# Hybrid decoder layer: products of ones before the first transposes, two tiles of x split straight from PSUM, memory's squares taken earlier

## The chip, the core and the metric

The kernel runs on one core of a Trainium2 chip. A core has TensorE (PE in the profile, with its weight loads as PEld), VectorE (DVE), ScalarE (ACT), GpSimd (POOL) and SyncE (SP, which here only issues DMAs). PE multiplies from the on-chip memory SBUF into the accumulators in PSUM; ACT and DVE read both; DMA moves data between SBUF and the chip's main memory. The metric is the device time of one execution in microseconds (us), the median of several.

## What is computed

One layer of a decoder on x (1024 tokens of 2048 channels, float32) with 256 memory tokens:

```python
h = rmsnorm(x, ln_g)
proj = h @ w_in                                   # split into 11 column groups
out_a = gmlp_spatial_gating(g_u, g_v, ...) * silu(g_z)
o = gated_delta_rule(q, k, v, g, beta)            # 8 heads, after a short causal convolution
out_b = rmsnorm(o, dn_norm_g) * silu(d_z)
m = rmsnorm(mem, mem_norm_g)
mk, mv = split(m @ w_mem_kv)                      # keys and values of memory, 4 heads x 128
out_c = softmax(c_q @ mk.T / sqrt(128)) @ mv * silu(c_z)
x = x + concat(out_a, out_b, out_c) @ w_out
y = rmsnorm(x, final_g)
```

## The kernel before

**Arithmetic.** Products that need float32 accuracy are made from pairs. A tensor is split into a high part, rounded to the fast type float32r by an ACT cast, and a low part, the difference taken by DVE (`split_to`, L440). A product is then three fast products, high x high, high x low and low x high (`triple`, L463). The split weights are called whi and wlo, the split normed x is ahi and alo: 16 tiles of 128 channels by 512 tokens, held as four tensors each (`ahq`, `alq`). A few small products and all transposes are done in plain float32.

**An order written by a planner.** The program does not issue instructions directly. Each call is recorded as an `Op` with an engine, a modelled cost and the ops that it must follow (L138). At the end `Plan.issue` (L228) simulates the five engines: whenever an engine is free it takes, among the ops that are ready by the model, the one with the lowest rank, and with equal ranks the one that stands first in the program. `rank(n)` sets the rank (default 5, products 9), `behind(op)` makes everything inside wait for an op. The result is a fixed order for each engine, which then runs in that order. All instructions are recorded by one helper, so the profile gives L295 for nearly every row; tiles are told apart by name.

**Two halves.** The sequence is treated in halves of 512 tokens, each of four tiles of 128 tokens. The first half's normed x is in ahi/alo from the start; the second half's is made later (`prep1`, L734), stored in main memory (`hT_d`), and loaded into ahi/alo when the first half's projections are over (`refill`, L1205). The raw first half is also kept in main memory (`h0_d`), because the later block products (a scheme that forms sums and differences of blocks and so needs seven block products instead of eight) use sums of the two halves: `left_sums` (L720) loads four raw 128x512 blocks into the ring zg, forms sums and differences on DVE and stores them to `s_d`.

**The first 70 us.** Memory's keys and values are computed first. Loads go out in this order: memory's rows (into tiles of the rings kT and qT), its norm gains, the weight rows of w_mem_kv (four buffers kvraw, made of the rings wraw and ut). A transpose turns the gains into a column (gcol, L532 to L536). Then 16 steps k follow (L580): ACT makes the scaled high part of the weights (whi, two buffers), DVE the low part (wlo), and PE runs 18 products, 12 of 256 columns into the four banks acc and 6 of 512 columns into two banks of dn. Memory's rows are transposed as they are, four channel tiles at a time (`spread_mem`, L537); their norm is a row factor rm, applied at the end. It comes from `row_scale` (L472): four squares with accumulation on ACT, all written to the one scrap tile jk, two small DVE ops, and a power on POOL. It is called for both memory tiles at k = 5, behind tile 0 of x.

Between the steps the four x tiles of the first half are prepared by `prep` (L548): row_scale, then for each quarter of the channels a DVE multiplication by scale and gains (gb, which lie in the ring zg), four PE transposes into one of two PSUM banks (`spare`, L528), and `put0` (L564), which copies the bank to a tile of the ring tn on ACT (rank 1), splits that copy into ahq and alq (rank 2), and stores it to `h0_d` (rank 6). Tiles 0, 1 and 2 are prepared at k = 5, 9 and 13, tile 3 after the last step.

**After that.** `project_first` (L836) makes the first projection, the tokens of tiles 0 and 1 first. Then each convolution of a head (`conv`, L860) runs one projection of 48 products of 512 columns, evacuates it, and takes a tile of the ring tn for a tanh on ACT. At each such convolution one job is taken from the list `todo` (`next_job`, L845): four `prep1`, which each take four tn tiles (`keep_rows`, L559), then four `left_sums`. Eight convolutions (heads 0 to 3, q and k) empty these eight jobs; four value projections and then `refill` follow. The ring tn has four tiles, handed out in the order of the program.

Of the kernel before, what the change touches and what calls it, by code (L numbers as in the profile page):

```python
# [12 lines left out]
ALU = mybir.AluOpType  # L13
# [4 lines left out]
P = 128  # L18
D = 2048
KT = D // P  # L20
# [3 lines left out]
NT = HT // P  # L24
# [36 lines left out]
class Plan:  # L61
# [27 lines left out]
    @contextmanager  # L89
    def rank(self, cls):  # L90
        old, self.cls = self.cls, cls
        yield
        self.cls = old

    @contextmanager
    def behind(self, op):
        old, self.gate = self.gate, op
        yield
        self.gate = old
# [199 lines left out]
def kernel(  # L299
# [21 lines left out]
    x, mem, w_in, out = x[0], mem[0], w_in[0], out[0]  # L321
# [7 lines left out]
    V, S, G, PE, Q = R.dve, R.act, R.pool, R.pe, R.sp  # L329
    rank, behind = R.rank, R.behind  # L330

    def C(shape, name, dt=F32):
        return sb.tile(list(shape), dt, name=name, tag=name)[:]

    def DT(shape, name, dt=F32):
        return dr.tile(list(shape), dt, name=name, tag=name)[:]
# [41 lines left out]
    def tok(ap):  # L378

        return ap.rearrange("p (t c) -> p t c", c=P)  # L380
# [3 lines left out]
    ahq = [C([P, NT, 4, P], f"ahi{q}", F32R) for q in range(NQ)]  # L384
    alq = [C([P, NT, 4, P], f"alo{q}", F32R) for q in range(NQ)]
    for t in (*ahq, *alq):
        R.users[t.tensor.name] = []
    ahi = [ahq[k // 4][:, :, k % 4] for k in range(KT)]
    alo = [alq[k // 4][:, :, k % 4] for k in range(KT)]
# [9 lines left out]
    ring = {t: Slots(t, 4, [P, HT]) for t in ("kT", "qT", "vs", "kd", "ai")}  # L399
# [13 lines left out]
    turn = {"acc": 0, "tp": 0, "dn": 0}  # L413
# [5 lines left out]
    def tpb():  # L419
        turn["tp"] += 1  # L420
        return acc[2 + turn["tp"] % 2]

    h0_d = DT([KT, P, HT], "h0d")
    hT_d = DT([KT, P, HT], "hTd")


    ident, ones, utri = (C([P, P], n) for n in ("ident", "ones", "utri"))
    G.memset(ident, 0.0)
    G.affine_select(out=ident, in_=ident, compare_op=ALU.not_equal, fill=1.0, base=0,
                    pattern=[[-1, P]], channel_multiplier=1)  # L430
    G.memset(ones, 1.0)
    mhalf = C([P, 8], "mhalf")
    G.memset(mhalf, -0.5)

    def rsqrt_to(o, a):
        with rank(1):
            G.tensor_tensor(out=o, in0=a, in1=mhalf[:, : a.shape[1]], op=ALU.pow)


    def split_to(hi, lo, src, eng):  # L440
        S.copy(hi, src)
        eng.tensor_tensor(out=lo, in0=src, in1=hi, op=ALU.subtract)
# [29 lines left out]
    def row_scale(xq):  # L472

        s = small()
        for c in range(4):
            S.activation(jk, xq[c], AF.Square, accum_out=s[:, c : c + 1])
        V.tensor_reduce(s[:, 4:5], s[:, 0:4], axis=AX.X, op=ALU.add)
        V.tensor_scalar(s[:, 4:5], s[:, 4:5], 1.0 / D, EPS, op0=ALU.mult, op1=ALU.add)
        rsqrt_to(s[:, 5:6], s[:, 4:5])
        return s[:, 5:6]  # L480


    def row_tiles(tag):
        if tag in ("inv", "gt", "ut"):
            return [b[:, i * HT : (i + 1) * HT] for b in (ring[tag](), ring[tag]()) for i in range(2)]
        return [ring[tag]() for _ in range(4)]
# [3 lines left out]
    mem_rows = [row_tiles("kT"), row_tiles("qT")]  # L490
# [6 lines left out]
    def kv_parts(k):  # L497
        n = XW if k == 0 else 2 * XW
        return [slice(i, i + n) for i in range(0, 2 * XW, n)]

    def load_kv(k):
        for sl in kv_parts(k):
            Q.dma_start(kvraw[k % 4][:, sl], w_mem_kv[k * P : (k + 1) * P, sl])

    def load_x(tt, tag, after=(None,) * 4):
        x_rows[tt] = row_tiles(tag)
        for c in range(4):
            with behind(after[c] or R.gate):
                Q.dma_start(x_rows[tt][c], x[tt * P : (tt + 1) * P, c * HT : (c + 1) * HT])
# [18 lines left out]
    def spare():  # L528
        turn["dn"] = 1 - turn["dn"]
        return flip[turn["dn"]]  # L530

    pt = spare()  # L532
    PE.transpose(pt[:, 0:16], mrow, ident[0:16, 0:16])
    gcol = C([P, 16], "gcol")
# [24 lines left out]
    def keep_rows(dst, q, tt, tp):  # L559
        t = ring["tn"]()  # L560
        S.copy(t, tp.rearrange("p t c -> p (t c)"))
        Q.dma_start(dst[4 * q : 4 * q + 4, :, tt * P : (tt + 1) * P].rearrange("k p n -> p k n"), tok(t))

    def put0(tt):  # L564
        def put(q, tp):
            t = tok(ring["tn"]())
            with rank(1):
                S.copy(t, tp)
            with rank(2):
                split_to(ahq[q][:, tt], alq[q][:, tt], t, V)  # L570
            with rank(6):
                Q.dma_start(h0_d[4 * q : 4 * q + 4, :, tt * P : (tt + 1) * P].rearrange("k p n -> p k n"), t)

        return put


    rm = []
    kvmark = []
    mhl = [spread_mem(0)]
    for k in range(KT):  # L580
        mh, ml = mhl[k // 4]
        if k >= 4:
            with rank(3):
                load_kv(k)
        hi, lo = kvhi[k % 2], kvlo[k % 2]
        with rank(2):
            for sl in kv_parts(k):
                raw = kvraw[k % 4][:, sl]
                S.activation(hi[:, sl], raw, AF.Copy, scale=gcol[:, k : k + 1])
                V.scalar_tensor_tensor(lo[:, sl], raw, gcol[:, k : k + 1], hi[:, sl], op0=ALU.mult, op1=ALU.subtract)  # L590
        kk = k % 4
        for h in range(NX):
            sl = slice(h * P, (h + 1) * P)
            triple(ka[h][:, :NMEM], (hi[:, sl], lo[:, sl]), (mh[:, kk], ml[:, kk]), k == 0, k == KT - 1)
        for mt in range(2):
            sl = slice(mt * P, (mt + 1) * P)
            triple(va[mt], (mh[:, kk, sl], ml[:, kk, sl]), (hi[:, XW:], lo[:, XW:]), k == 0, k == KT - 1)
        kvmark.append(R.ops[-1])
        if k == 3:
            with rank(2), behind(kvmark[-1]):  # L600
                for c in range(4):
                    Q.dma_start(gb[c], ln_g[0, c * HT : (c + 1) * HT].partition_broadcast(P))
        if k in (1, 4, 8):
            with behind(kvmark[-1]):
                mhl.append(spread_mem(len(mhl)))
        if k == 1:
            load_x(0, "vs", kvmark[1:2] * 4)
        if k == 4:
            load_x(1, "kd", kvmark[4:5] * 4)
        if k == 5:  # L610
            prep(0, put0(0), spare)
            for mt in range(2):
                rm.append(C([P, 1], f"rm{mt}"))
                V.tensor_copy(rm[mt], row_scale(mem_rows[mt]))
        if k == 7:

            dg, rmb = (ring["E"]()[:, 0:NMEM] for _ in range(2))
            for mt in range(2):
                V.tensor_scalar(dg[:, mt * P : (mt + 1) * P], ident, rm[mt], None, op0=ALU.mult)
            pt = spare()  # L620
            PE.matmul(pt[:, 0:NMEM], ones, dg, start=True, stop=True)
            S.copy(rmb, pt[:, 0:NMEM])
        if k == 9:
            prep(1, put0(1), spare)
            load_x(2, "kT", (kvmark[6], kvmark[7], kvmark[7], kvmark[8]))
        if k == 13:
            load_x(3, "qT", (kvmark[10], kvmark[11], kvmark[11], kvmark[12]))
            with rank(2):
                prep(2, put0(2), spare)
# [6 lines left out]
    for mt in range(2):  # L636
        t = [ring["ai"](F32R) for _ in range(2)]
# [9 lines left out]
    for h in range(NX):  # L647
        t = ring["vs"](F32R).rearrange("p (s m) -> p s m", s=2)
# [48 lines left out]
    NJ = NH // 2  # L697
# [19 lines left out]
    def blk(w, k, c0):  # L717
        return w[k * P : (k + 1) * P, c0 : c0 + HT]

    def left_sums(j):  # L720
        a, b, c, d = (ring["zg"]() for _ in range(4))
        with rank(6):
            for t, x_ in zip((c, d, a, b), (hT_d[j], hT_d[NH + j], h0_d[j], h0_d[NH + j])):
                Q.dma_start(t, x_)
            V.tensor_tensor(out=d, in0=c, in1=d, op=ALU.add)
            Q.dma_start(s_d[0][j][0], d)
            V.tensor_tensor(out=c, in0=a, in1=c, op=ALU.subtract)
            Q.dma_start(s_d[0][j][2], c)
            V.tensor_tensor(out=d, in0=d, in1=a, op=ALU.subtract)
            Q.dma_start(s_d[0][j][1], d)  # L730
            V.tensor_tensor(out=b, in0=b, in1=d, op=ALU.subtract)
            Q.dma_start(s_d[0][j][3], b)

    def prep1(i):  # L734
        load_x(NT + i, "ut")
        prep(NT + i, lambda q, tp: keep_rows(hT_d, q, i, tp), over(scan_banks))
# [77 lines left out]
    todo = []  # L814
# [379 lines left out]
    decays(0, a)  # L1194
    R.late = R.LATE
    todo += [lambda i=i: prep1(i) for i in range(NT)]
    todo += [lambda j=j: left_sums(j) for j in range(NJ)]
    gdrs = [front(0, 0, (first, None)), front(1, 0)]
    for h in range(NJ):
        early_values(h, 0)  # L1200
# [4 lines left out]
    def refill(k):  # L1205

        raw = wraw()
        with rank(2):
            Q.dma_start(raw, hT_d[k])
            split_to(ahi[k], alo[k], tok(raw), V)  # L1210

    a = tpb()

    def before(k):
# [369 lines left out]
    for n, (tag, to) in enumerate((("gt", mkT), ("inv", mv))):  # L1584
        for i in range(NX // 2):
            t = ring[tag](F32R).rearrange("p (h s m) -> p h s m", h=2, s=2)
# [103 lines left out]
    tn = ring["tn"].bufs  # L1690
# [86 lines left out]
```

## Time and profile before

| | |
|---|---|
| median of 3 runs | 1633.85 us (1631.82 to 1637.55) |
| the profiled execution, time | 1636.6 us |
| the profiled execution, span | 1634.8 us |
| PE busy | 1611.6 us |
| DVE busy | 1259.3 us |
| ACT busy | 1029.1 us |
| mean granted PE clock | 0.997 |
| mean DMA rate over the span | 262 GB/s |

The span runs from the first to the last instruction of the core; the time of the execution holds a little more. Busy time of PE is the union of its products' modelled durations. They overlap: a product of 512 columns lasts 0.39 us in the trace while the next one starts 0.23 us after it, so how fast PE goes is read from the distance between starts. In the timeline a row gives the start, the duration, the engine, the operation, the tiles (out<-in), the shape, how many were merged, and in brackets how long the engine had been idle and what ended that. A view by windows gives busy microseconds of each engine, the number of instructions, the granted clock, and the share and rate of DMA.

### The profile page before, as it was taken

To read this page: it belongs to the slowest core of one execution; us is meant where nothing else is said; L and a number is where in the kernel's file an instruction comes from. 1 tells how busy PE (TensorE), PEld (TensorE's weight loads), DVE (VectorE), ACT (ScalarE), POOL (GpSimd) and SP (SyncE) were. 2 spreads that over 40 slices of the span, in tenths; PEclk is the share of its full clock that TensorE was granted. 3 is DMA by queue.
4 is the path that set the end of the run, shared out by engine and by line. 5 is a ranking of instruction groups with operands and counts; after the bars stand their busy time and mean duration, and the time that the engine had idled before them with its cause. 6 is when DMAs were issued, how large, how long until landed. Compare 5 with 4: busy or idle time off the path is not lost.

```text
span 1634.8 us, 26073 instructions
## 1 busy us (share of the span) xinstructions
PE 1611.6 (99%) x8562; PEld 1353.0 (83%) x8562; DVE 1259.3 (77%) x2082; ACT 1029.1 (63%) x2223; POOL 292.1 (18%) x482
## 2 busy tenths in 40 slices
PE   8999999999999999999999999999999999999997
PEld 7888888887788888888788888888888888888886
DVE  5866777878865567899898897777768888689775
ACT  6867765765365556888685356765666784344345
POOL 0011310461341110223135014231000000000001
PEclk9999999999999999999999999999999999999999
DMA  9977897899967886589878977878968879688646
GB/s 315 258 219 208 264 293 229 262 306 292 353 231 232 279 286 197 189 301 342 288 242 277 304 226 245 266 263 293 323 218 267 266 227 361 203 270 299 216 145 241
DMA packets 279146, 428.93 MB, mean 262 GB/s; under 512 B 30889, under 2 KB 104162, under 8 KB 279010
## 3 DMA queue, kind: packets, MB, share of 16 engines
q1 hardware_dynamic: 256258, 366.81, 68.4%
q0 software_dynamic: 22144, 59.40, 11.8%
q8 instruction: 67, 1.10, 0.3%
q10 hardware_dynamic: 608, 1.06, 0.2%
q14 instruction: 69, 0.57, 0.1%
HBM read 339.57 MB, written 87.06 MB: 261 GB/s over the span
## 4 chain that ended last, share of the span: by engine, by line
PE 88%; DMA 7%; ACT 2%; DVE 2%; issue 1%; SPq 0%; POOLq 0%; POOL 0%; ACTq 0%; DVEq 0%
PE acc L295 67%; PE dn L295 20%; DMA y<-in_w_in_dram 1%; DMA wraw<-in_w_in_dram 1%; ACT whi L295 1%; DMA raws<-h0d 1%; DMA ut<-in_x_dram 0%; DVE wlo L295 0%; DMA kd<-in_w_in_dram 0%; ACT jk L295 0%; DMA el<-vd 0%; DMA qT<-in_w_in_dram 0%; DMA kT<-in_w_in_dram 0%; DMA wraw<-in_w_mem_kv_dram 0%; DMA kT<-in_x_dram 0%
## 5 line engine op out<-in xcount | busy, mean ns | idle before, releaser
L295 PE MATMUL acc<-ahi,whi 128*128 128x512 f32 (+1 forms) x1512 | 534.9, 392 | 2.1 <-ACT whi L295 2.1
L295 PE MATMUL acc<-ahi,wlo 128*128 128x512 f32 (+1 forms) x1144 | 447.9, 391 | 1.0 <-DVE wlo L295 1.0
L295 PEld LDWEIGHTS acc<-ahi,whi 128*128 128x128 f32 x1512 | 283.2, 189 | 57.4 <-ACT whi L295 3.0
L295 PE MATMUL acc<-alo,whi 128*128 128x512 f32 (+1 forms) x776 | 302.2, 389 | 0.0
L295 PEld LDWEIGHTS acc<-ahi,wlo 128*128 128x128 f32 x1144 | 215.6, 188 | 42.5 <-DVE wlo L295 1.2
L295 ACT CAST whi<-wraw 128x512 fp32r<-128x512 f32 (+1 forms) x167 | 133.7, 804 | 135.1 <-PE acc L295 92.7
L295 DVE TENSOR_TENSOR wlo<-wraw,whi 128x512 fp32r<-128x512 f32 (+1 forms) x167 | 153.7, 922 | 62.8 <-ACT whi L295 60.1
L295 ACT CAST ahi<-raws 128x1024 fp32r<-128x1024 f32 x130 | 136.3, 1049 | 68.6 <-PE acc L295 24.9
L295 PEld LDWEIGHTS acc<-alo,whi 128*128 128x128 f32 x776 | 146.0, 188 | 27.4
L295 PE MATMUL acc<-ahi,zh 128*128 128x512 f32 x376 | 149.0, 396 | 0.3 <-ACT vs L295 0.3
L295 PE MATMUL acc<-ahi,zl 128*128 128x512 f32 x376 | 149.3, 397 | 0.0
L295 PE MATMUL acc<-alo,zh 128*128 128x512 f32 x376 | 149.1, 397 | 0.0
L295 POOL TENSOR_TENSOR small<-small,mhalf 128x1 f32<-128x1 f32 x26 | 17.1, 662 | 586.7 <-DVE small L295 586.7
L295 DVE TENSOR_TENSOR alo<-y,ahi 128x1024 fp32r<-128x1024 f32 x65 | 79.8, 1227 | 18.7 <-ACT ahi L295 18.6
L295 ACT CAST ahi<-y 128x1024 fp32r<-128x1024 f32 x65 | 68.2, 1049 | 39.7 <-PE dn L295 15.8
L295 DVE TENSOR_TENSOR ahi<-raws,ahi 128x1024 fp32r<-128x1024 f32 x65 | 79.8, 1227 | 16.1 <-ACT ahi L295 15.2
L295 DVE TENSOR_TENSOR alo<-raws,ahi 128x1024 fp32r<-128x1024 f32 x65 | 79.3, 1220 | 15.3 <-ACT ahi L295 14.6
L295 PEld LDWEIGHTS acc<-ahi,zh 128*128 128x128 f32 x376 | 71.0, 189 | 13.9 <-ACT vs L295 0.6
L295 PEld LDWEIGHTS acc<-alo,zh 128*128 128x128 f32 x376 | 71.0, 189 | 13.5
L295 PEld LDWEIGHTS acc<-ahi,zl 128*128 128x128 f32 x376 | 71.0, 189 | 13.4
L295 PE MATMUL acc<-whi,ahi 128*128 128x512 f32 x232 | 80.1, 392 | 0.0
L295 PE MATMUL dn<-whi,ahi 128*128 128x512 f32 x216 | 74.1, 389 | 0.0
(416 smaller groups left out, 3398.2 us busy)
## 6 DMA issues: line engine op xcount, KB each, us to landing
wraw<-in_w_in_dram SPq DMA_DIRECT2D x268, 256.0 KB, 4.3
raws<-sd SPq DMA_DIRECT2D x150, 256.0 KB, 4.0
y<-in_w_in_dram SPq DMA_DIRECT2D x92, 256.0 KB, 4.5
y<-sd SPq DMA_DIRECT2D x75, 256.0 KB, 3.9
wraw<-in_w_out_dram SPq DMA_DIRECT2D x64, 256.0 KB, 5.2
raws<-h0d SPq DMA_DIRECT2D x54, 256.0 KB, 5.5
y<-in_w_out_dram SPq DMA_DIRECT2D x33, 256.0 KB, 4.4
sd<-zg SPq DMA_DIRECT2D x32, 256.0 KB, 4.9
```

What stands on the lines that cost most here:

```text
L295: o.fn(*o.args, **o.kw)
```

## The change

```diff
+    G.memset(ones, 1.0)
     G.memset(ident, 0.0)
     G.affine_select(out=ident, in_=ident, compare_op=ALU.not_equal, fill=1.0, base=0,
                     pattern=[[-1, P]], channel_multiplier=1)
-    G.memset(ones, 1.0)
...
+    def warm(n):
+        t = spare()
+        for _ in range(n):
+            PE.matmul(t[:, 0:P], ones, ones, start=True, stop=True)
+
+    turn["dn"] = 1
+    warm(7)
     pt = spare()
     PE.transpose(pt[:, 0:16], mrow, ident[0:16, 0:16])
...
+    H0 = NT // 2
+
     def put0(tt):
         def put(q, tp):
+            if tt >= H0:
+                with rank(1):
+                    split_to(ahq[q][:, tt], alq[q][:, tt], tp, V)
+                return
             t = tok(ring["tn"]())
...
-            with rank(6):
+            with rank(5):
                 Q.dma_start(h0_d[4 * q : 4 * q + 4, :, tt * P : (tt + 1) * P].rearrange("k p n -> p k n"), t)
...
+        if k == 3:
+            for mt in range(2):
+                rm.append(C([P, 1], f"rm{mt}"))
+                V.tensor_copy(rm[mt], row_scale(mem_rows[mt]))
...
         if k == 5:
             prep(0, put0(0), spare)
-            for mt in range(2):
-                rm.append(C([P, 1], f"rm{mt}"))
-                V.tensor_copy(rm[mt], row_scale(mem_rows[mt]))
...
+    def whole(k):
+        t = ring["tn"]()
+        with rank(4):
+            V.tensor_tensor(out=tok(t)[:, H0:], in0=ahi[k][:, H0:], in1=alo[k][:, H0:], op=ALU.add)
+            Q.dma_start(h0_d[k][:, H0 * P :], t[:, H0 * P :])
+
     def left_sums(j):
         a, b, c, d = (ring["zg"]() for _ in range(4))
-        with rank(6):
+        with rank(5):
...
-    todo += [lambda j=j: left_sums(j) for j in range(NJ)]
+    todo += [lambda j=j: [*(whole(k) for k in range(j, KT, NJ)), left_sums(j)] for j in range(NJ)]
...
+    while todo:
+        todo.pop(0)()
     a = tpb()
```

Seven float32 products of the 128x128 tile of ones with itself are put first on PE, into a PSUM bank that nothing reads, and the memset of ones goes ahead of that of the identity. Tiles 2 and 3 of x are no longer copied to tn and stored: `split_to` reads the PSUM bank itself, at rank 1. Their raw values are formed later, channel tile by channel tile, as the sum of the high and the low part (`whole`), in the four jobs that also hold the first four `left_sums`, four tiles in each, and stored as 128 rows of 256 values. The squares and scales of memory's rows stand at k = 3 instead of behind x's tile 0 at k = 5. The stores of tiles 0 and 1 and the work of `left_sums` have rank 5 instead of 6. A loop before the second half takes whatever is left in the list of jobs.

## Prediction, made before the changed kernel was run

> **What bounds the kernel now.** I read the page first, then the windows of the first 70 us, and the timelines of PE, ACT and DVE there.
>
> ```profile
> span 1634.8 us, 26073 instructions
> ...
> PE 1611.6 (99%) x8562; PEld 1353.0 (83%) x8562; DVE 1259.3 (77%) x2082; ACT 1029.1 (63%) x2223; POOL 292.1 (18%) x482
> ```
>
> PE is busy for 1611.6 of 1634.8 us, so only 23.2 us are open to any change that leaves the products alone, unless PE is slow while busy. The change works in the first 70 us and on the sums at 160 to 220 us. The windows (busy us of PE, PEld, DVE, ACT, POOL, then clock, DMA share, GB/s) show where the early holes are:
>
> ```profile
> 0.00:5.00 5.00, 0.48 (x2) 0.40 (x3) 0.17 (x1) 1.28 (x1) 1.36 (x9) 1.00 0.48 152
> ...
> 10.00:15.00 5.00, 5.00 (x27) 4.53 (x27) 2.05 (x2) 1.44 (x2) 0.00 (x0) 1.00 1.04 408
> 15.00:20.00 5.00, 5.00 (x36) 4.54 (x35) 3.01 (x4) 2.55 (x4) 0.00 (x0) 1.00 0.96 322
> ...
> 55.00:60.00 5.00, 4.17 (x29) 3.33 (x29) 4.39 (x8) 5.00 (x12) 0.28 (x1) 1.00 0.94 266
> 60.00:65.00 5.00, 4.84 (x34) 4.19 (x33) 4.59 (x7) 5.00 (x11) 0.00 (x0) 1.00 0.70 199
> 65.00:70.00 5.00, 3.97 (x29) 3.59 (x28) 5.00 (x12) 4.61 (x12) 0.92 (x1) 1.00 0.37 92
> ```
>
> Two things matter. From 10 to 15 us PE is full with 27 instructions, from 15 to 20 with 36: it is slow while busy. And from 55 to 70 us PE lacks 2.0 us while ACT is full and then DVE.
>
> **Term 1, the seven products of ones.** PE's timeline shows the slowness:
>
> ```profile
> 3.73 0.26 PE L295 MATMUL dn<-ident,y 16*128 16x16 f32 x1 [3.73 <-DMA y<-in_mem_norm_g_dram]
> ...
> 4.78 1.12 PE L295 MATMUL dn<-ident,kT 128*128 128x128 f32 x4 [0.79 <-DMA kT<-in_mem_dram]
> ...
> 7.67 1.22 PE L295 MATMUL acc<-gt,whi 128*128 128x256 f32 x4 [0.92 <-ACT gt L295]
> ...
> 10.32 1.28 DVE L295 SCALAR_TENSOR_TENSOR wlo<-wraw,gcol,whi 128x1024 fp32r<-128x1024 f32 x1 [1.13 <-ACT whi L295]
> ...
> 10.61 0.41 PE L295 MATMUL acc<-gt,wlo 128*128 128x256 f32 x1
> 10.82 0.41 PE L295 MATMUL acc<-inv,whi 128*128 128x256 f32 x1
> ...
> 12.10 0.63 PE L295 MATMUL dn<-wlo,gt 128*128 128x512 f32 x1
> 12.53 0.48 PE L295 MATMUL dn<-whi,inv 128*128 128x512 f32 x1
> ...
> 13.80 0.28 PE L295 MATMUL acc<-gt,wlo 128*128 128x256 f32 x1
> 13.92 0.28 PE L295 MATMUL acc<-gt,whi 128*128 128x256 f32 x1
> ...
> 15.44 0.39 PE L295 MATMUL dn<-whi,inv 128*128 128x512 f32 x1
> 15.67 0.60 PE L295 MATMUL dn<-ident,kT 128*128 128x128 f32 x4
> ```
>
> Before 12.53 a product of 256 columns starts 0.21 us after the last one and one of 512 columns 0.43; afterwards 0.12 and (15.44 to 15.67) 0.23. The clock column says 1.00 there, but the pitch says half. The same pitch of 0.43 comes back at 389 us, and there the column shows 0.50:
>
> ```profile
> 387.60 0.50 PE L295 MATMUL acc<-ahi,whi 128*128 128x512 f32 x1 [1.96 <-ACT whi L295]
> 388.39 0.79 PE L295 MATMUL acc<-ahi,zh 128*128 128x512 f32 x1 [0.28 <-ACT vs L295]
> ...
> 390.68 0.63 PE L295 MATMUL acc<-ahi,zl 128*128 128x512 f32 x1
> 391.11 0.62 PE L295 MATMUL acc<-ahi,whi 128*128 128x512 f32 x1
> ...
> 388.20:391.50 3.30, 3.11 (x7) 2.37 (x8) 3.16 (x8) 0.65 (x2) 0.57 (x1) 0.50 0.90 288
> ```
>
> So PE runs at half clock after idling, and needs about 3.3 us of work to leave that state. Seven f32 products of 128 columns are fourteen PE instructions: the four such products of L1185 stand as eight in the trace. The memset of ones is POOL's second now:
>
> ```profile
> L295 PE MATMUL dn<-wsT,ones x8: 271/273/275, 216.8 to 223.6; 128*128 128x128 f32 x8
> ...
> 0.95 0.20 POOL L295 MEMSET ones<- 128x128 f32 x1
> ```
>
> Four f32 transposes of the same width take 1.12 us at half clock, about 0.24 from start to start, so the fourteen take 3.3 us. They need only that memset (0.20 us, then the first), start near 1.1 and end near 4.4. Cover: PE waits until 3.73 for the row of gains and until 4.78 for memory's rows. The gains' transpose comes about 0.7 us later; the first user of gcol is ACT at 6.42, its copy ran at 4.02, so 1.7 us of cover remain. Without cover the cost would be that 0.7.
>
> What full clock buys: step 0 (18 products) starts at 7.67 as before, since ACT's casts end then, and its twelve short and six long products at 0.12 and 0.23 are 2.8 us; waiting for its second half of weights, it ends near 10.7 instead of 12.9. Step 1 is then held: its third product needs wlo, done at 10.32 + 1.28 = 11.60, and ten short and six long remain: 1.2 + 1.4 us, ending at 14.2 instead of 15.67. Gain 1.4. The upper bound is an order with all wlo products last (2.2). The lower bound is 0, should the gate not open earlier. The load for step 2 landed by 13.05 at the latest; if only then, 0.9. I take 1.4.
>
> The Trainium skill (TensorE: Matmul & The Clock Gate, Part 1) says that the array leaves half clock after a busy window of about 3.4 us and that this window runs free of the kernel. The trace agrees with the length (3.3 us at 388); by the free window the gain would differ from run to run. The same page (Part 4) says that transposes do not count as busy in the same way, which speaks against this change, since eight transposes stand between the ones and the first real product. By that rule the gate opens 3.3 us after 7.67, near 11.0, and term 1 would be about 0.7. No row here separates the two.
>
> **Term 2, the end of memory's stage.** PE's holes there, with what ended them, and ACT's groups from 40 to 68 us:
>
> ```profile
> 56.75 0.66 PE L295 MATMUL dn<-ident,kT 128*128 128x128 f32 x4 [0.23 <-ACT tn L295]
> ...
> 58.84 0.38 PE L295 MATMUL acc<-gt,whi 128*128 128x256 f32 x1 [0.60 <-ACT whi L295]
> ...
> 61.12 0.75 PE L295 MATMUL acc<-gt,wlo 128*128 128x256 f32 x4 [0.15 <-DVE wlo L295]
> ...
> 67.31 0.39 PE L295 MATMUL acc<-ahi,wlo 128*128 128x256 f32 x1 [1.03 <-DVE wlo L295]
> ...
> L295 ACT COPY tn<-dn 128x512 f32<-128x512 f32 x8 | 4.7, 583 | 0.0
> ...
> 25.89 0.63 ACT L295 ACTIVATE jk<-kT 128x512 bf16<-128x512 f32 x1
> ...
> 41.26 0.66 ACT L295 ACTIVATE jk<-qT 128x512 bf16<-128x512 f32 x1
> ```
>
> The idle times add up to 2.01 us; each also loses the overlap of a product with the next (0.28 long, 0.12 apart), so 2.01 + 4 x 0.16 = 2.65 us. ACT is full from 55 to 65. The change takes from it, before 67 us, four of those eight copies (the others are tile 1's, which stay): 4 x 0.58 = 2.3 us. Four more, of tile 3, go after 67. It also moves memory's eight squares. They ran between 25.89 and 41.9, behind tile 0's, because all squares write the one tile jk; a square with its accumulator read is 0.75 us, eight are 6.0. Ahead of x's they can run from about 10 to 22 us, where the windows 10:15 and 15:20 leave ACT 3.56 + 2.45 = 6.0 us. Behind a square on ACT stand the casts whi, and a cast with its wlo takes 1.15 + 1.28 of a step's 2.8, so up to 0.3 us of slack per step hides them; uncovered, 0.4 a step over four steps, 1.6.
>
> DVE is not relieved: it splits the same tiles, now from PSUM, and 65:70 is full. A bank is held until DVE is done, 0.63 + 0.69 instead of 0.58 us, over two banks: nothing while other products fill PE, up to 8 x 0.74 / 2 = 3.0 us if they do not. So term 2 lies between +3.0 (loss) and -2.65; since ACT's relief of 8.3 us is three times the holes and DVE has room before 50 us, I take -2.2.
>
> **Term 3, the raw values later.** Added: sixteen DVE sums of 256 columns, near the 0.42 us of the same form from PSUM (below), 6.7 us; sixteen stores of 128 KB, the same bytes as the eight removed, on SP at about 0.4 us each to issue. They land at 160 to 200 us, where PE has no hole; DVE is the fuller engine and DMA is full at its end (window 190:200; then two tanh and the landing row of the tile hTd from 100 to 200 us):
>
> ```profile
> L295 DVE TENSOR_TENSOR xr<-acc,E 128x256 f32<-128x256 f32 x4 | 1.4, 417 | 0.0
> ...
> 190.00:200.00 10.00, 10.00 (x51) 8.53 (x50) 9.08 (x23) 8.57 (x28) 3.20 (x5) 1.00 1.06 308
> ...
> 171.30 0.62 ACT L295 ACTIVATE tn<-qT 128x512 f32<-128x512 f32 x1
> ...
> 186.06 0.63 ACT L295 ACTIVATE tn<-kT 128x512 f32<-128x512 f32 x1 [0.66 <-DVE kT L295]
> ...
> DMA to landing us min/median/max: 2.9/6.6/8.5
> ```
>
> I take 0: the cover is PE's queue of projections. Without it the price is rival C's. The ranks 6 to 5 let tile 0's and 1's stores pass x's rows: 0 to +1, taken as 0. The loop that empties the jobs finds none left: eight jobs, eight convolutions before it. Memory's row_scale keeps its other instructions.
>
> **Sum:** -1.4 - 2.2 + 0 = -3.6 on a span of 1634.8, so 1631.2; this execution took 1636.6 in all, 1.8 around its span, and lies 2.75 above the median. Against the median of 1633.85 that is 1630.2.
>
> **Rivals.**
> A, the forecast: 1630.2, own range 1627.5 to 1633. About 0.3%, 4.9 us, is what a measurement here can tell, so the line lies at 1628.95, and a third of A is beyond it.
> B, a later hole closes too. At 387.60 PE waits 1.96 + 0.28 us and then runs eight long products at 0.43 instead of 0.23 (1.6), near 4 us with the overlap. What is late is one load of weights, in a chain row that stands 9.13 us:
>
> ```profile
> 377.30 9.13 DMA y<-in_w_in_dram
> ```
>
> Every instruction after the change is dealt anew by modelled times, so that load may meet other traffic. Against it: the shift of the whole is uniform, and the tile rings are handed round by multiples of four, so the order there may be the same. With the 1.4 and 2.2: 1626.
> C, slower. The sums of raw values take tn tiles, four per job, between the tanh of one convolution and the next. A tanh then waits for an add and a store: 0.42 + 6.6 = 7.0 us a group by the landing row (its view holds 16 stores of the same kind and 4 loads), 28 for four groups, where the trace has 14.8 between 171.30 and 186.06. ACT takes instructions in order, so the casts of weights stand behind a waiting tanh. Of the 13 us, two pieces of weights of 2.8 us each are lead; 7.6 remain: 1630.2 + 7.6 = 1638. It decides once one wait on ACT exceeds the lead. For it: DMA share 1.06 at 190. Against: four earlier jobs use tn in the same way.
> D, the ones do not open the gate early: -2.2 alone, 1631.7, within the line.
>
> **Numbers.** A 0.42, B 0.30, C 0.18, D 0.10. Faster: 0.14 + 0.30 = 0.44; within: 0.28 + 0.10 = 0.38; slower: 0.18. The range runs from 1623.5, below most of B, to 1638, half of C.
>
> **What would show it.** Term 1: a pitch of 0.12 at 8 to 10 us, the first mem transposes of step 1 near 14.2. Term 2: no idle rows of PE at 55 to 68, ACT below full there, memory's squares before 22. Term 3: PE full at 160 to 220, no ACT tanh with a long wait on a store. Wrong would be: half clock until 12, a hole before the second half of the first projection (banks), a hole near 180.

## The result: 0.31% slower, and the profile after

| | before | changed |
|---|---|---|
| median of 17 runs | 1634.29 us (1629.25 to 1637.55) | 1639.00 us (1635.26 to 1642.28) |
| ratio, 95% interval | | 1.0031 (1.0022 to 1.0040) |
| the profiled execution, time | 1636.6 us | 1637.68 us |
| the same program profiled again | 1632.0 us | 1639.19 us |

The change costs 4.7 us where 3.6 were to be gained. The two profiled executions lie only 1.1 us apart, because that of before is 2.3 us above its median and that of the changed kernel 1.3 below. So each program was profiled a second time (the runs same_as_before and same_as_after below), and what follows rests on both.

The page of the changed kernel, span and busy times:

```profile
span 1636.0 us, 26138 instructions
...
PE 1613.5 (99%) x8576; PEld 1353.7 (83%) x8576; DVE 1262.9 (77%) x2098; ACT 1024.6 (63%) x2215; POOL 291.8 (18%) x482
```

The first stage does become shorter. Its windows (busy us of PE, PEld, DVE, ACT, POOL, then clock, DMA share, GB/s):

```profile
0.00:5.00 5.00, 3.95 (x17) 3.69 (x18) 0.17 (x1) 2.00 (x3) 1.33 (x9) 1.00 0.53 159
...
10.00:15.00 5.00, 4.99 (x34) 4.34 (x33) 2.14 (x2) 2.30 (x6) 0.00 (x0) 1.00 1.04 409
15.00:20.00 5.00, 4.66 (x31) 4.04 (x31) 3.14 (x7) 4.97 (x11) 0.55 (x1) 1.00 1.03 400
...
30.00:35.00 5.00, 3.95 (x28) 3.23 (x26) 2.95 (x4) 2.80 (x7) 0.00 (x0) 1.00 1.01 392
...
55.00:60.00 5.00, 5.00 (x38) 4.54 (x37) 4.75 (x8) 3.58 (x8) 0.00 (x0) 1.00 0.98 293
60.00:65.00 5.00, 5.00 (x35) 4.54 (x34) 5.00 (x12) 4.85 (x13) 0.53 (x1) 1.00 0.40 102
65.00:70.00 5.00, 5.00 (x45) 5.00 (x44) 4.56 (x8) 2.44 (x8) 0.93 (x3) 1.00 0.97 281
```

From 10 to 15 us PE now starts 34 instructions instead of 27, and from 55 to 70 us it has no hole (the second profile has 4.82 busy at 60 to 65). New ones stand at 15 to 20, where ACT is full, and at 30 to 35. PE's timeline in the same stage:

```profile
1.05 3.36 PE L295 MATMUL dn<-ones 128*128 128x128 f32 x14 [1.05 <-POOL ones L295]
4.34 0.28 PE L295 MATMUL dn<-ident,y 16*128 16x16 f32 x1
4.55 1.11 PE L295 MATMUL dn<-ident,kT 128*128 128x128 f32 x4
...
8.63 0.28 PE L295 MATMUL acc<-inv,whi 128*128 128x256 f32 x1
8.75 0.28 PE L295 MATMUL acc<-gt,wlo 128*128 128x256 f32 x1
...
13.59 0.60 PE L295 MATMUL dn<-ident,kT 128*128 128x128 f32 x4
...
35.10 0.66 PE L295 MATMUL dn<-ident,vs 128*128 128x128 f32 x4 [1.14 <-ACT tn L295]
```

The pitch (the distance from start to start) is 0.12 from 8.63 on, and the transposes that stood at 15.67 stand at 13.59. The new hole of 1.14 us belongs to tile 0 of x, whose copies still go through ACT. ACT's timeline shows why the copy is late:

```profile
32.20 0.63 ACT L295 ACTIVATE jk<-kd 128x512 bf16<-128x512 f32 x1 [3.56 <-DMA kd<-in_x_dram]
...
34.48 0.56 ACT L295 COPY tn<-dn 128x512 f32<-128x512 f32 x1
```

In the planned order a square of tile 1 of x (kd) stands ahead of this copy, and ACT waits 3.56 us for tile 1's rows to land. How long the lead lasts is seen from the start of the n-th product of 512 columns (n from 0, all 6016 counted in the trace, us; the later rows are experiments):

| kernel | n = 100 | 1100 | 2000 | 5800 |
|---|---|---|---|---|
| before | 81.4 | 339.1 | 598.2 | 1577.3 |
| before, again | 80.0 | 338.3 | 594.2 | 1572.8 |
| changed | 78.3 | 336.5 | 598.2 | 1577.9 |
| changed, again | 78.6 | 337.1 | 597.3 | 1579.5 |
| e_late_after | 79.1 | 336.7 | 595.1 | 1575.6 |
| e_late_before | 79.3 | 336.9 | 592.0 | 1571.8 |
| y_late_before | 80.6 | 339.6 | 600.4 | 1579.9 |

Three executions have the changed first part and four the old one: the means are 336.8 and 338.5 at n = 1100, a lead of 1.7 us, though one of the four (336.9) lies among the three. From there to n = 2000 the two of before take 259.1 and 255.9, the two of the changed kernel 261.7 and 260.2: 3.5 more on average, where the two of before alone differ by 3.2. From 2000 to 5800 it is 2.1 more (979.7 and 982.2 against 979.1 and 978.6), and the work behind PE's last product takes 8.9 us instead of 8.4. Together -1.7 + 3.5 + 2.1 + 0.5 = 4.4, near the 4.7 of the medians.

Where the 3.5 goes is shown by the changed kernel's timelines of SP, POOL, ACT and PE around 387 us:

```profile
375.12 0.85 SPq L295 DMA_DIRECT2D y<-in_w_in_dram  x2
...
375.08 1.51 POOL L295 DMA_DIRECT2D E<-gcd  x2 [3.06 <-DVE alo L295]
...
386.82 1.04 ACT L295 CAST whi<-y 128x1024 fp32r<-128x1024 f32 x1 [7.54 <-DMA y<-in_w_in_dram]
...
387.92 0.50 PE L295 MATMUL acc<-ahi,whi 128*128 128x512 f32 x1 [1.86 <-ACT whi L295]
390.12 1.12 PE L295 MATMUL acc<-ident,tn 128*128 128x128 f32 x4 [1.70 <-DVE tn L295]
```

and by the same place before:

```profile
376.87 0.85 SPq L295 DMA_DIRECT2D y<-in_w_in_dram  x2
...
377.31 1.52 POOL L295 DMA_DIRECT2D E<-gcd  x2 [2.61 <-DVE alo L295]
...
386.50 1.04 ACT L295 CAST whi<-y 128x1024 fp32r<-128x1024 f32 x1 [3.43 <-DMA y<-in_w_in_dram]
```

It is the place of rival B, the late weights of the first block product. Two issues on SP bring the two halves of these weights (y); two on POOL spread a row of decays over all partitions (E, line 908 of the kernel before, two heads of the delta rule). Before, the first E goes out 0.44 us behind the first load, about with the second one; ACT can cast 9.6 us after the first issue. After, the first E goes out 0.04 us ahead of both loads, and ACT can cast after 11.7 us. ACT takes its instructions in the planned order: it stands idle for 7.54 us, and a tanh behind the cast, with DVE's step behind that, then holds PE a second time (1.70). From 388.94 to 395.77 us the granted clock is 0.50. The windows from 380 to 400 us show the loss as fewer instructions of PE; changed, then before (its second execution had 19.66 busy and x90, the changed kernel's second 16.34 and x66):

```profile
380.00:400.00 20.00, 16.44 (x62) 12.98 (x61) 13.04 (x26) 5.84 (x10) 1.75 (x4) 0.83 0.77 248
```
```profile
380.00:400.00 20.00, 17.76 (x75) 13.98 (x74) 15.28 (x29) 8.84 (x16) 2.27 (x5) 0.91 0.87 260
```

### The profile page after: what moved, and what is told of

Read it like the earlier page. It is cut to its first block, busy times and chain, and to the rows that moved or that the text cites. A ratio compares the mean times of both kernels' runs of the same rounds, so it can differ in the third digit from the quotient of the medians.

```text
span 1636.0 us, 26138 instructions
## 1 busy us (share of the span) xinstructions
PE 1613.5 (99%) x8576; PEld 1353.7 (83%) x8576; DVE 1262.9 (77%) x2098; ACT 1024.6 (63%) x2215; POOL 291.8 (18%) x482
## 3 DMA queue, kind: packets, MB, share of 16 engines
q0 software_dynamic: 22144, 59.40, 11.7%
## 4 chain that ended last, share of the span: by engine, by line
PE 83%; DMA 8%; DVE 4%; ACT 2%; issue 1%; POOL 1%; SPq 0%; POOLq 0%; DVEq 0%; ACTq 0%
PE acc L295 63%; PE dn L295 20%; DMA y<-in_w_in_dram 2%; DMA wraw<-in_w_in_dram 2%; DVE wlo L295 1%; DMA wraw<-hTd 1%; DMA raws<-h0d 1%; DMA y<-h0d 1%; DVE y L295 1%; DMA kT<-in_mem_dram 0%; DMA kd<-in_x_dram 0%; SPq L295 0%; DMA ut<-in_x_dram 0%; ACT whi L295 0%; DMA pd<-y 0%
```

## Experiments

Two groups of four kernels were run to ask whether one part of the change costs the time or the order that is dealt anew. Three theories: **G**, the lead is given back at the hole of 387 us whatever the order; **S**, the late sums of raw values cost it; **O**, any new dealing of the order behind some 240 us moves the time by several us. A third group tests O's sharpened form **H** (E's transfers, issued ahead, hold the weights back) against **K** (the weights are late from all the traffic together).

**p_warm: before, with the products of ones alone.**

```diff
+    G.memset(ones, 1.0)
     G.memset(ident, 0.0)
...
+    turn["dn"] = 1
+    warm(7)
     pt = spare()
```

> Before plus the seven products of ones alone (with the memset moved). Theory G (the early gain is real and is given back at the change of phase near 387 us, where a load of weights lands at a time that PE's lead does not move): PE is 1.4 us ahead of before's profile at 300 us, the product behind the hole still starts near 387.6, total within 1.5 us of before. Rival S (the raw values' sums and stores cost the time): 1.4 us faster than before, since they are not in it. Rival O (any new order of the planner after 240 us moves the time by several us, whatever the early part does): a time up to 5 us off before in either direction that the early lead doesn't explain.

Measured: 1638.41 us, ratio 1.0029 (1.0015 to 1.0042).

**p_squares: before, with memory's squares at k = 3.**

```diff
+        if k == 3:
+            for mt in range(2):
+                rm.append(C([P, 1], f"rm{mt}"))
+                V.tensor_copy(rm[mt], row_scale(mem_rows[mt]))
...
-            for mt in range(2):
```

> Before plus the move of memory's squares alone. Theory G: some 1 to 2 us ahead at 300 us, given back at 387, total within 1.5 us of before. Rival S: 1 to 2 us faster than before in the end. Rival O: up to 5 us off in either direction.

Measured: 1639.14 us, ratio 1.0029 (1.0019 to 1.0038).

**p_split: before, with the split from PSUM and the late sums, rank 6 kept.**

```diff
+            if tt >= H0:
+                with rank(1):
+                    split_to(ahq[q][:, tt], alq[q][:, tt], tp, V)
+                return
...
+    todo += [lambda j=j: [*(whole(k) for k in range(j, KT, NJ)), left_sums(j)] for j in range(NJ)]
```

> Before plus the split of tiles 2 and 3 from PSUM and the later sums alone (ranks stay 6). Theory G: about 1 us ahead at 300 us, total within 1.5 us of before. Rival S: 4 to 6 us slower than before, with holes of PE between 160 and 260 us or loads of the sums landing later near 370 us. Rival O: up to 5 us off in either direction, with holes after 380 us at new places.

Measured: 1642.42 us, ratio 1.0051 (1.0035 to 1.0068).

**p_ranks: before, with rank 5 for the two ranks 6, no instruction added or removed.**

```diff
-            with rank(6):
+            with rank(5):
...
-        with rank(6):
+        with rank(5):
```

> Before plus rank 5 for 6 in the stores of h0d and in left_sums alone; no early lead is in it. Theory G: within 1.5 us of before. Rival S: the same. Rival O: up to 5 us off, from an order that differs only where the sums stand.

Measured: 1639.46 us, ratio 1.0038 (1.0023 to 1.0054).

Each part alone is at least as slow as the whole, even the one that changes nothing but two ranks; over the 1634.72 us of before in this set the four would cost 20.6 us if added up, where the whole costs 4.7. S falls as the one cause, since three of the four hold no late sums; G falls in its plain form, since the parts aren't equal to before, and p_warm isn't ahead as G expected: its product n = 1100 starts at 343.2. O stands, but p_split's 7.7 us are more than its 5, and all four orders lose, which O doesn't explain. The four don't lose in one place. The windows of p_ranks and of p_squares that lack most (before has 20.00 busy in the first and 40.00 and 37.76 in the others):

```profile
340.00:360.00 20.00, 17.86 (x81) 14.63 (x80) 14.40 (x28) 11.64 (x37) 13.09 (x23) 0.91 0.80 233
```
```profile
720.00:760.00 40.00, 38.43 (x180) 31.76 (x179) 35.90 (x58) 33.20 (x68) 13.13 (x17) 1.00 0.95 325
760.00:800.00 40.00, 36.55 (x175) 29.60 (x174) 35.65 (x55) 29.51 (x68) 8.09 (x10) 1.00 0.89 288
```

**f_late_before and f_late_after: the first part of one kernel, the later order of the other.** From the second half of the sequence on, each engine's order is set by the times that the other kernel's plan had given; the former is the changed kernel with before's late order, the latter before with the changed late order.

```diff
+    R.mark = len(R.ops)
     a = tpb()
...
+        at = np.cumsum(np.frombuffer(zlib.decompress(base64.b85decode(ORDER)), np.int32)) + SHIFT
...
+        for o, w in zip(made[self.mark :], at):
+            key[o] = float(w)
```

> The changed kernel's first part with before's order kept, engine by engine, for everything that is recorded from the second half of the projections on (issued from about 205 us). Theory O (the new order of the instructions between some 205 and 640 us costs the time, and the early lead is real): the early lead of 3 to 4 us stays, about 1631. Theory G (the lead is lost at 387 us, whatever the order): 1634 to 1636, with the hole at 387 longer by the lead. Rival S (the raw values' sums cost it): 1638 to 1640, like the changed kernel.

Measured: 1640.99 us, ratio 1.0043 (1.0026 to 1.0060).

> Before's first part with the changed kernel's order for everything recorded from the second half of the projections on. Theory O: slower than the changed kernel, which has the early lead besides, 1641 to 1643. Theory G: 1634 to 1636 as before. Rival S: 1634 to 1636, since the sums are not in it.

Measured: 1642.33 us, ratio 1.0052 (1.0035 to 1.0068).

Both are slow, and the pair can't be read by its time: where the two orders meet, both got holes that neither kernel has. In the window from 200 to 260 us, where before is busy for 60.00 and the changed kernel for 59.94, f_late_after has 57.14 and f_late_before has this:

```profile
200.00:260.00 60.00, 54.05 (x258) 43.95 (x258) 43.41 (x84) 36.59 (x103) 10.56 (x17) 1.00 0.90 286
```

The place at 387 us is as asked, though: f_late_after has E ahead of the weights, as the changed kernel has, and loses as much there.

```profile
380.00:400.00 20.00, 15.78 (x64) 12.49 (x64) 14.21 (x27) 6.77 (x13) 3.90 (x7) 0.88 0.91 299
```

**same_as_before and same_as_after: both programs once more.** Each is given its own order by the same table that the pair above uses, so every engine's order stays as it was.

> Before's own program once more, for a second profile: every theory expects the time of before, 1630 to 1637, and the profile shows which of before's holes come back in another execution (the half clock at 388 and 449 us above all).

Measured: 1632.94 us, ratio 0.9993 (0.9983 to 1.0004).

> The changed program once more, for a second profile: every theory expects 1635 to 1642; the profile shows which holes of the changed kernel come back.

Measured: 1637.07 us, ratio 1.0028 (1.0013 to 1.0044).

**e_late_after, e_late_before, e_late_warm: the two E transfers later.** In the changed kernel, in before and in p_warm only these two issues of POOL are moved, behind its next memset of xr; every other instruction of every engine keeps its place.

```diff
         self.ops.sort(key=lambda o: (o.at, o.idx))
+        order = self.ops
+        pool = lambda o, n: o.eng == "pool" and o.fn.__name__ == n
+        e = [i for i, o in enumerate(order) if pool(o, "dma_start") and "gcd" in o.args[1].tensor.name][8:10]
+        m = next(i for i in range(e[1], len(order)) if pool(order[i], "memset"))
+        moved = [order[i] for i in e]
+        order[e[0] : m + 1] = [o for o in order[e[0] : m + 1] if o not in moved] + moved
```

> The changed kernel with every engine's order as it was, but the two POOL transfers E<-gcd that stood ahead of the two loads of weights (y<-in_w_in_dram, about 375 us) put behind POOL's next MEMSET of xr (about 382.5 us). Theory H (these two transfers, issued ahead, hold the weights back): the second load of weights lands 7 to 9 us after its issue instead of 11.3, the time that PE loses at 380 to 400 us falls from 6.7 (5.8 in the second look) to 3 or less, and the kernel takes 1633 to 1635.5 us, within 0.1% of before. Rival K (the weights are late because of all that is under way, h0d's parts and gt's blocks among it, and E's place is a coincidence): landing still 10.5 to 11.5 us, 5 us or more lost, 1637 to 1640.

Measured: 1634.40 us, ratio 1.0006 (0.9995 to 1.0018). The timelines of SP, POOL and ACT, and two windows:

```profile
375.31 0.85 SPq L301 DMA_DIRECT2D y<-in_w_in_dram  x2
...
382.85 1.51 POOL L301 DMA_DIRECT2D E<-gcd  x2
...
380.88 1.05 ACT L301 CAST whi<-y 128x1024 fp32r<-128x1024 f32 x1 [1.47 <-DMA y<-in_w_in_dram]
```
```profile
380.00:382.00 2.00, 2.00 (x11) 1.65 (x10) 2.00 (x5) 1.05 (x1) 0.00 (x0) 1.00 1.04 406
...
380.00:400.00 20.00, 20.00 (x92) 16.57 (x91) 19.38 (x35) 10.39 (x15) 3.23 (x6) 1.00 0.99 314
```

The cast starts 5.6 us after the first load's issue instead of 11.7 (sooner than the 7 to 9 us to the landing that H expected), PE has no hole left from 380 to 400 us, and the ratio falls from 1.0031 (and 1.0028 in the second set) to 1.0006: 0.22 to 0.25%, or 3.6 to 4.1 us. The interval of 1.0031 doesn't overlap with the new one; that of the second set (from 1.0013) does a little.

> The kernel before with the same two E<-gcd transfers (issued 10 to 20 ns behind the second load of weights) put behind POOL's next MEMSET of xr (about 384 us); nothing else is moved. H: the weights land in 6 to 7.5 us rather than 7.3 to 9.2, PE loses 1 us or less at 380 to 400 us (before: 4.3 in one execution, 1.0 in another), and the time is 0 to 2.5 us under the kernel before. K: as before in all, within 1 us.

Measured: 1632.58 us, ratio 0.9996 (0.9984 to 1.0008). Cast after 6.1 us, PE 20.00 busy with x94. Here the place had cost less, and the gain is within what can't be told from none, so the time alone fits K too: no version that beats before was found.

> The kernel before with the products of ones alone (1638.4 before this edit, 4.0 us lost at 380 to 400 us, weights landed 8.8 us after issue with E<-gcd 10 ns behind them), and the two E<-gcd transfers put behind POOL's next MEMSET of xr. H: loses 1.5 us or less there, 1635 to 1636.5. K: unchanged, 1638 to 1639.

Measured: 1633.44 us, ratio 1.0003 (0.9991 to 1.0016), against p_warm's 1.0029. Cast after 6.1 us instead of 9.2, PE 20.00 busy with x94 instead of 18.19 with x76. It gained more than H expected. Its profiled execution was the slowest of its 12, 1639.5, so the trace tells only of this place.

**y_late_before: the converse.** Before, with its two loads of weights put behind two other loads into y on SP, so that E goes out 0.46 us ahead of them.

```diff
+        y, h = ([order[i] for i in near if s in order[i].args[1].tensor.name][:2] for s in ("in_w_in", "h0d"))
+        m = order.index(h[1])
+        i = order.index(y[0])
+        order[i : m + 1] = [o for o in order[i : m + 1] if o not in y] + y
```

> The converse: the kernel before with its two loads of weights put behind the two loads y<-h0d in SP's order, so that they are issued some 0.9 us later, at about 377.8 and 378.2 us, behind the two E<-gcd transfers (377.3 and 378.1) instead of ahead of them. H: the second load lands 10.5 us or more after its issue, at 388.5 us or later, PE loses 5 us or more at 380 to 400 us, and the time is 1636 to 1639. K: landing only 0.9 us later than before's 384 to 386.5, 1 us more lost, 1633.5 to 1635.5.

Measured: 1639.36 us, ratio 1.0035 (1.0022 to 1.0048). The timelines of SP, POOL, ACT and PE, and the window:

```profile
378.76 0.90 SPq L303 DMA_DIRECT2D y<-in_w_in_dram  x2
...
378.30 1.51 POOL L303 DMA_DIRECT2D E<-gcd  x2 [2.61 <-DMA raws<-h0d]
...
390.01 1.04 ACT L303 CAST whi<-y 128x1024 fp32r<-128x1024 f32 x1 [5.95 <-DMA y<-in_w_in_dram]
...
391.11 0.79 PE L303 MATMUL acc<-ahi,whi 128*128 128x512 f32 x1 [4.48 <-ACT whi L303]
```
```profile
380.00:400.00 20.00, 15.52 (x60) 12.04 (x59) 12.98 (x27) 5.16 (x12) 2.19 (x5) 0.83 0.82 251
```

Two loads moved by 0.9 us against E make before as slow as the changed kernel: the cast waits 11.3 us from the first issue, and PE's hole is 4.48. The two loads now also stand behind the two others on SP, so part of their wait may come from those; that wasn't separated. By the time of the cast H holds in all four kernels of this group, K in none.

## Why the prediction was wrong

**The step that failed** is the one that let the lead run to the end: "the shift of the whole is uniform, and the tile rings are handed round by multiples of four, so the order there may be the same". It wasn't. The planner dealt E ahead of the weights, and the load named in rival B came later still. ACT could cast 11.7 us after the first load's issue instead of 9.6, and 5.6 with E out of the way. B had the place right and the sign wrong: it asked whether the load could meet less traffic, not more. No rival held a loss there; the one on the slow side, C, was put in another place.

**Term 1** (-1.4): the ones took 3.36 us from 1.05, as worked out, and memory's transposes of step 1 stand 2.08 us earlier, near the upper bound of 2.2, since the pitch was 0.12 soon after step 0's start. But this pair flatters the ones. The profile of before, from which the sum started, has these transposes later than any other execution without the ones: eight such stand between 14.43 and 15.67, 15.04 on average. Six with the ones stand between 13.39 and 15.02, 14.05 on average, so they bring 1.0 on average. In two of the six the clock was half again; this is p_warm:

```profile
7.40:10.80 3.40, 3.40 (x14) 3.19 (x15) 2.28 (x4) 1.87 (x2) 0.00 (x0) 0.50 0.97 340
```

There the same transposes start at 14.63; in e_late_after, with half clock from 8.25 to 11.66, at 15.02. The prediction cited the Trainium skill (TensorE: Matmul & The Clock Gate, Part 1) for windows of 3.4 us that run free of the kernel; this row agrees, with 3.4 us at half clock behind seven products of ones.

**Term 2** (-2.2): the holes at 55 to 68 us closed, ACT fell from 5.00 to 3.58 in the window at 55, and memory's squares ended before 22, as said. What was missed is what ACT does when these squares are out of its way: it comes to tile 1's squares before their rows of x have landed, and waits for them with tile 0's copies behind it. That made the hole of 1.14 us at 35.10. p_squares, which has this move alone, shows the same waits of ACT and then of PE, and longer:

```profile
33.64 0.63 ACT L295 ACTIVATE jk<-kd 128x512 bf16<-128x512 f32 x1 [4.54 <-DMA kd<-in_x_dram]
...
36.54 0.66 PE L295 MATMUL dn<-ident,vs 128*128 128x128 f32 x4 [2.12 <-ACT tn L295]
```

In before, p_warm and p_split, which lack the move, neither wait is there. With both terms the shown pair leads by 2.6 us at n = 1100, and all seven executions by 1.7 on average, where 3.6 were summed. The terms don't add, either. At n = 100, some 80 us, six executions with before's first part stand between 79.3 and 81.4 (mean 80.3) and four with the changed one between 78.3 and 79.1. Those with a single part have no lead there: 81.0 and 81.7 with the ones (p_warm, e_late_warm), 81.7 in p_squares, 82.7 in p_split.

**Term 3** (0) was right at its place, and rival C's mechanism wasn't seen: PE is busy for 40.00 of 40 us from 160 to 200 and for 59.94 of 60 from 200 to 260.

**D** (ones without effect) has the outcome of the ones alone, though not by its reason: in e_late_warm the transposes stood at 13.39, earliest of all, and the lead was gone by n = 100. By time, E's place moves p_warm by 0.26% and hides what the ones bring; with E late, the kernel with the ones and the one without differ by less than either interval. What the ones bring inside the whole change wasn't tried.

**What stays open.** With E late in both, the changed kernel should lead by its first part's 1.7 us; it reads 1634.40 against 1632.58, ratios whose intervals overlap. So of the 4.7 us between the two kernels E's place accounts for about 2.9. From the forecast of -3.6 to the measured 4.7 it is 8.3 us: 1.9 by a lead that was smaller, 2.9 by E's place, and some 3.5 whose cause isn't shown. The trace of e_late_after loses time at 420 to 460 us instead, on the chain of the triangular inverse (PE busy 57.55 of 60 from 400 to 460 at a clock of 0.94, e_late_before 58.05 at 0.97), which one execution of each can't establish. What makes p_squares, p_split and p_ranks slow later on wasn't tried either; the lost windows above name places, not causes.

## What to carry to other kernels

Where a planner deals the order anew, a gain at the front can be lost to transfers that change places behind it; look up the longest DMA row of the chain of waits first and list what is issued within 1 us of it on the other queues. A change of a few us is better judged after such a collision is taken away in both kernels, and from more than one profiled execution: the single pair of profiles shows the ones' gain at about twice its mean. An engine relieved of work that it does in order may only arrive earlier at a load that hasn't landed. A transfer that isn't needed soon should be issued behind a load that PE waits for.

## What was not expected of the hardware

**POOL's transfers against SP's loads.** Time from the first issue of the weights to ACT's cast: 5.6, 6.1 and 6.1 us with E 7.5 to 7.7 us behind it; 7.7 to 9.6 us in five profiles with E about with the second load (before twice, p_warm, p_squares, f_late_before); 11.3 to 12.3 us in five with the first E ahead of both (changed twice, p_split, f_late_after, y_late_before). One profile with E ahead, p_ranks, had 9.0, so the order isn't all of it. Some 3 to 7 us behind E's issue the rate of all DMA falls. The changed kernel's windows there, which stand against 406 GB/s in e_late_after from 380 to 382:

```profile
378.00:380.00 2.00, 2.00 (x10) 1.65 (x9) 1.93 (x5) 1.25 (x2) 0.63 (x1) 1.00 0.67 150
380.00:382.00 2.00, 2.00 (x10) 1.69 (x9) 2.00 (x5) 0.00 (x0) 0.00 (x0) 1.00 0.84 156
```

Before has 124 and 143 GB/s from 380 to 384 us, and e_late_after, with E at 382.85, has 201 and 197 from 386 to 390. Other transfers of POOL are under way in these windows, so that E lowers the rate isn't shown.

The Trainium skill (DMA: Bandwidth & Descriptors, Queues, rings and completion order) has each DMA engine take turns between the queues that have work, packet by packet. E's 512 KB (two issues of 256 KB in the page's list of issues) beside the weights' 512 KB would then, as an estimate, about double the weights' time, which agrees in size with 11.7 us against 5.6. Why the rate of all falls to 150 GB/s, no run here shows.

**Spread between executions.** The same program of before lost 20.00 - 17.76 = 2.2 us of PE's time at 380 to 400 us in one execution and 0.3 in another, with the same order of issue.
